# Moving a fifth of the dense experts' first products from the key loop to the end of the trunk

## The chip, the core and the metric

The kernel runs on one NeuronCore of a Trainium2 chip. TensorE (PE) multiplies matrices, VectorE (DVE) and ScalarE (ACT) do the element-wise work, GpSimd (POOL) issues the gathers, and the queue of SyncE (SP) issues most other transfers; 16 DMA engines carry them between the device memory (HBM) and on-chip memory. The metric is the device time of one execution in microseconds.

## The reference

One step of a hybrid layer over 9 tiles of 128 tokens (8 tiles of a prompt, one of decode samples), model width 1024. Cut to the part that matters here:

```python
x = x + mixer(rmsnorm(x, g_mix), ...)          # gating unit + retention: "the trunk"
t = rmsnorm(x, g_ffn)
q = (t @ w_query).reshape(T, 8, 256)           # 8 heads
s1, s2 = q[..., :128] @ k1.T, q[..., 128:] @ k2.T     # scores over 128 first and 128 second keys
v1, i1 = top_k(s1, 16); v2, i2 = top_k(s2, 16)
cand = (v1[..., :, None] + v2[..., None, :])          # 16 x 16 sums, of these the best 16
vals, flat = top_k(cand, 16)
experts = e1 * 128 + e2                        # one of 16384 single-neuron experts
w = softmax(vals)
a = gelu(einsum('td,thkd->thk', t, eu[experts]))      # first product, with u
out = einsum('thk,thkd->td', w * a, ev[experts])      # second product, with v
x = x + out;  y = rmsnorm(x, g_final)
```

## The kernel before

A tile framework takes the program as written, with priorities, and lays each engine's instructions out in one fixed order; every engine then runs its own list in order and waits on semaphores. [...]

**Trunk.** The tiles run in three groups (`GROUPS`, L48). `order` (L92 to L106) lists the 128 weight units of 512 x 256 for each group. `take` (L127 to L142) hands the next unit to the products: it keeps three raw loads ahead (`load`, L115 to L124, queued on SP) and splits each unit into a high and a low part, a cast on ACT and a subtraction on DVE (`split`, L197 to L206), since every product is the sum of three products of parts. The last step of a group is `query` (L597 to L630), 8 heads of scores; between the heads it runs `ahead`, the preparation of the next group's input, of which there is none for the last group.

**Experts, in two ways.** Tiles 0, 1, 2, 6 and 7 are *gathered*: for each of a token's 128 chosen experts an indirect DMA (L791) fetches the rows of u and v, DVE forms the dot product (L752), ACT the GELU and weight (L757, L758), DVE accumulates (L762). That is 640 gathers of 1 MB, through five buffers `gat`. Tiles 3, 4, 5 and 8 are *dense*: for each of the 128 second keys e all 128 experts of that key are computed for all 512 tokens. For this `expand` (L797 to L848) turns a tile's 128 choices per token into a full 128 x 128 table of weights: per four tokens one comparison on DVE (L828), four steps split between DVE (L838) and ACT (L842, L843) by `AA` (tokens 1 and 3 of four on DVE), four matmuls (L818), a copy to the buffer `st` (L819), and after four such chunks a 1 MB store of `st` to the spill `pdr` (L821). `st` is one buffer.

**The order around the change.** `advance(c)` moves a side clock by the matmul time just issued and lets two side lanes run up to it: the lane of gathers, one gather per `PACE` us, and the lane of top-16 and expansion (`topk_units`, L665 to L746), which after the trunk has priority. When the trunk is through, the four dense tiles are transposed to `tT` (L931 to L941), then the side lanes run until tile 8 is expanded (L942 to L944). Only then do the trunk's buffers close and the key loop begins (L1005 to L1047). For each key e it multiplies u of that key with `tT` into `S` (24 matmuls of 512 columns, L1014), takes GELU (L1019), multiplies by the weights `pt` (L1021, loaded from `pdr` for eight keys at a time, L1009), splits the result into `g`, splits u of key e + 2 and v of key e, and runs 24 matmuls of 512 columns with v (`res` and `blk`, L985) for the key before. Raw u and v pass through one ring of four slots `wraw` (L962 to L965). The block sums are added in L994.

Of the kernel before, what the change touches and what calls it, by code (L numbers as in the profile page):

```python
# [44 lines left out]

EARLY = [0, 1, 2, 8]
TD = len(DENSE) * P
EC = 4  # L48
LT = 16
BE = 8  # L50
# [4 lines left out]
def step_kernel(ctx: ExitStack, tc: tile.TileContext, x, state, wall, wst, bs, rows, vec, cst, smp, cosd, sind, euv,  # L55
# [37 lines left out]
    for g in range(len(GROUPS)):  # L93
# [10 lines left out]
            order += [U_IN + 2 * (32 + cb), U_IN + 2 * (32 + cb) + 1, U_PA + 2 * cb, U_PA + 2 * cb + 1]  # L104
        order += [U_OUT + i for i in range(8)] + [U_Q + i for i in range(16)]
    per = len(order) // len(GROUPS)  # L106
    NRAW, NPART, NBK = 3, 3, 2
    GB = 5
    MIX = 3
# [5 lines left out]
    def load(n):  # L115
        nonlocal pair
        if n < per - 2 and n % 3 < 2:

            if n % 3 == 0:
                pair = peer.tile([P, 2, 4, 256], F32, name="gat", bufs=GB)  # L120
            t = pair[:, n % 3]
        else:
            t = wp.tile([P, 4, 256], F32, name="wraw", bufs=NRAW)
        nc.sync.dma_start(t, wall[order[n]])  # L124
        return t

    def take():  # L127
# [94 lines left out]
    def front(gi, pl):  # L222

        tl = GROUPS[gi]
        nt = len(tl)
        xt = pl.tile([P, nt, D], F32, name="xt")
        ss = pl.tile([P, 4], F32, name="fss")
        junk = pl.tile([P, D], BF16, name="fjunk")
        for i, t in enumerate(tl):
            nc.sync.dma_start(xt[:, i], x[t])  # L230
        yield
        for i in range(nt):
            nc.scalar.activation(junk, xt[:, i], AF.Square, accum_out=ss[:, i:i + 1])
            rstd_of(ss[:, i:i + 1], ss[:, i:i + 1], D, epst)
            nc.scalar.activation(xt[:, i], xt[:, i], AF.Copy, scale=ss[:, i:i + 1])
            if i % 2:
                yield
        hT = hTs[gi] = pair_tiles(act, nt * P, "h")
        for k in range(KD):
            ps = sp.tile([P, 512], F32, name="sps")  # L240
            for i in range(nt):
                tr(ps[:, i * P:(i + 1) * P], xt[:, i, k * P:(k + 1) * P], ident)
            split([t[:, k] for t in hT], ps[:, :nt * P], vc[:, C_GMIX + k:C_GMIX + k + 1])
            if k % 2:
                yield

    def trunk(gi):
        tl = GROUPS[gi]
# [348 lines left out]
    def query(gi, pl, tl, nt, T, tT, rs, unit):  # L597
        def scores(h, qh):
            for i, t in enumerate(tl):
                ps = sp.tile([P, 2, P], F32, name="sps")  # L600
                for c in range(2):
                    mm(ps[:, c], qh[:, c, i * P:(i + 1) * P], sk[c], start=True, stop=True)
                st = pl.tile([P, 2, P], F32, name="st", bufs=2 * nt)
                nc.scalar.activation(st, ps, AF.Copy, scale=rs[:, i:i + 1])
                st = st.rearrange("p a b -> p (a b)")
                if t in EARLY:
                    top_keys(t, h, st)
                else:
                    store(ssp[t][:, h], st, 1)

        prev = None
        ahead = front(gi + 1, pl) if gi + 1 < len(GROUPS) else iter(())
        next(ahead, None)
        for h in range(PH):
            qh = pl.tile([P, 2, T], F32, name="qh", bufs=2)
            unit = unit or gemm_f(tT, T, U_Q + 2 * h)
            nc.scalar.copy(qh, (yield from unit))
            unit = None
            if prev:
                scores(*prev)  # L620
# [12 lines left out]
    BOOST = [100]  # L633
    AB = 2
    EUB, RWB = 2, 4
    AA = (1, 3)
    BB = (1, 0)
    EXC = 4
    DP = 200
# [157 lines left out]
    def expand(t):  # L797
# [27 lines left out]
        for c in range(P // EC):  # L825
            ab = ex.tile([P, 2, EC, P], F32, name="ab", bufs=AB)
            if c % BB[0] >= BB[1]:
                nc.vector.tensor_tensor(ab[:, 1], eT[:, 1, EC * c:EC * c + EC, None].to_broadcast([P, EC, P]),  # L828
                                        io[:, None, :].to_broadcast([P, EC, P]), op=OP.is_equal)
            else:  # L830
                for j in range(EC):
                    k = EC * c + j
                    nc.scalar.activation(ab[:, 1, j], io, AF.Square, scale=-1.0, bias=eT[:, 1, k:k + 1])
                nc.scalar.activation(ab[:, 1], ab[:, 1], AF.Relu, scale=-1.0, bias=1.0)
            for j in range(EC):
                k = EC * c + j
                if j % 4 in AA:
                    nc.vector.tensor_scalar(ab[:, 0, j], io, eT[:, 0, k:k + 1], eT[:, 2, k:k + 1],  # L838
                                            op0=OP.is_equal, op1=OP.mult)
                else:  # L840

                    nc.scalar.activation(ab[:, 0, j], io, AF.Square, scale=-1.0, bias=eT[:, 0, k:k + 1])  # L842
                    nc.scalar.activation(ab[:, 0, j], ab[:, 0, j], AF.Relu, scale=eT[:, 3, k:k + 1],  # L843
                                         bias=eT[:, 2, k:k + 1])
            if last:
                products(*last)
            last = c, ab
            yield EXC  # L848
# [67 lines left out]
    def advance(c):  # L916
        nonlocal tm
        tm += c
        flush()
        run_side(tm)  # L920
# [7 lines left out]
        ready.update(GROUPS[gi])  # L928


    prep = ExitStack()  # L931
    dx = prep.enter_context(tc.tile_pool(name="dx", bufs=2))
    tT = pair_tiles(act, TD, "h")
    for n, t in enumerate(DENSE):
        xt = dx.tile([P, D], F32, name="dx")
        nc.sync.dma_start(xt, tsp[t])
        for j in range(2):
            ps = sp.tile([P, 4, P], F32, name="sps")
            for k in range(4):
                tr(ps[:, k], xt[:, (4 * j + k) * P:(4 * j + k + 1) * P], ident)  # L940
            split([w[:, 4 * j:4 * j + 4, n * P:(n + 1) * P] for w in tT], ps)  # L941
    while len(expanded) < len(DENSE):  # L942
        tm += 1.0
        run_side(tm)  # L944
    prep.close()
    ex_sb.close()
    trunk_sb.close()
    trunk_ps.close()
# [12 lines left out]

    def fetch(name, e):  # L962
        if e < NKEYS:
            raw[name, e] = wp.tile([P, D], F32, name="wraw", bufs=RWB)
            nc.sync.dma_start(raw[name, e], eud[e].rearrange("p k e -> p (k e)") if name == "eu" else evd[e])  # L965

    def split_u(e):
        if e < NKEYS:
            eu[e] = [wp.tile([P, D], F32R, name=n, bufs=EUB) for n in ("whi", "wlo")]
            split(eu[e], raw.pop(("eu", e)))  # L970

# [22 lines left out]
            nc.vector.tensor_tensor(oacc[o], oacc[o], ps, op=OP.add)  # L994

    us = 24 * mm_us(TD)
    PACE[0] = 4.6
    todo = []
    hp = ExitStack()
    hp.enter_context(tc.high_priority(DP))  # L1000
# [4 lines left out]
    for e in range(NKEYS + 1):  # L1005
        if e < NKEYS:
            if e % BE == 0:
                pt = dp.tile([P, TD // LT, BE, LT], F32, name="pt", bufs=2)
                nc.sync.dma_start(pt.rearrange("p c e t -> p c (e t)"), pdr[e // BE])  # L1009
            ps = dps.tile([P, TD], F32, name="S")  # L1010
            for k in range(KD):
                w, a = [p[:, k * P:(k + 1) * P] for p in eu[e]], [p[:, k] for p in tT]
                for i, (x, y) in enumerate(((w[0], a[0]), (w[1], a[0]), (w[0], a[1]))):
                    mm(ps, x, y, start=k == 0 and i == 0, stop=k == KD - 1 and i == 2)  # L1014
            del eu[e]
            fetch("ev", e + 1)
            fetch("eu", e + 2)
            a = dp.tile([P, TD], F32, name="a", bufs=2)
            nc.scalar.activation(a, ps, AF.Gelu_apprx_tanh)  # L1019
            r16 = lambda z: z.rearrange("p (c t) -> p c t", t=LT)  # L1020
            nc.vector.tensor_tensor(r16(a), r16(a), pt[:, :, e % BE], op=OP.mult)  # L1021
            G[e] = [dp.tile([P, TD], F32R, name=f"g{m}", bufs=NBK + 1) for m in range(2)]
            split(G[e], a)
            split_v(e)
            split_u(e + 2)
            hp.close()
            advance(us)
            hp.enter_context(tc.high_priority(DP))
        if todo:
            block(*todo.pop())  # L1030
        if e:
            for o in held:
                value(res[o], o, e - 1, e == 1, e == NKEYS)
            if e % NBK == 0 or e == NKEYS:
                es = list(range((e - 1) // NBK * NBK, e))
                if len(blocked) > 0:
                    block(blocked[0], es)
                if len(blocked) > 1:
                    todo.append((blocked[1], es))
            hp.close()  # L1040
            advance(us)
            hp.enter_context(tc.high_priority(DP))
# [98 lines left out]
```

## Time and profile before

| | |
|---|---|
| median of 3 runs | 3904.63 us (3904.46 to 3918.01) |
| the profiled execution | 3911.42 us, span of its instructions 3909.7 us |
| busy in the span | PE 3583.4, DVE 3433.9, ACT 1838.5, POOL 986.5 us |
| DMA | 1176 MB, mean 301 GB/s |
| mean granted clock of PE | 0.962 of 2.4 GHz |

Times in the profile are microseconds from the span's start. An engine's busy time is the union of its instructions; a mean duration overlaps a little with the next instruction, so what one costs in a full stretch is read from start to start. "to landing" is the time from a DMA's issue to its last byte. Line numbers in the profile are those of the kernel before; the change shifts them by 4 in the weight stream, by 17 in the top-16 and the expansion, and by 30 in the key loop.

### The profile page before, as it was taken

How to read it: one execution, taken by the hardware profiler on the slowest of the kernel's cores; microseconds unless marked ns; L12 is line 12 of the kernel's file. 1: busy time of each engine (PE TensorE's matmuls, PEld its weight loads, DVE VectorE, ACT ScalarE, POOL GpSimd, SP SyncE). 2: the span in 40 equal slices, each digit the busy share in tenths (PEclk: the TensorE clock that was granted, in tenths of full speed). 3: DMA queues.
4: the chain of work that ended last, by engine and by line, in shares of the span. 5: the costliest groups of instructions: out<-in, count | busy, mean ns of one | idle time of the engine just before them, and what ended most of it. 6: DMA issues, size and time to landing. Idle time of an engine off the chain costs nothing.

```text
span 3909.7 us, 54608 instructions
## 1 busy us (share of the span) xinstructions
PE 3583.4 (92%) x19724; PEld 3060.1 (78%) x19724; DVE 3433.9 (88%) x6391; ACT 1838.5 (47%) x3839; POOL 986.5 (25%) x692
## 2 busy tenths in 40 slices
PE   8999999999999888889989836999999999999998
PEld 6789977887877787878989835777787777777776
DVE  5666799999988899899888897999999999899996
ACT  4445634444443545656666637343344343343443
POOL 0000002333433220221212221233223333333331
PEclk9999999999999999999999967999999999999999
DMA  8766547999989874685868965899789999999995
GB/s 313 248 238 200 179 161 297 377 343 349 364 315 361 343 273 145 238 288 182 296 213 310 315 240 199 326 381 370 274 317 367 391 376 386 346 388 373 380 383 187
DMA packets 243759, 1176.00 MB, mean 301 GB/s; under 512 B 26656, under 2 KB 43808, under 8 KB 159520
## 3 DMA queue, kind: packets, MB, share of 16 engines
q0 software_dynamic: 105216, 721.46, 49.5%
q1 hardware_dynamic: 138272, 451.04, 31.5%
q8 instruction: 155, 2.54, 0.3%
q14 instruction: 116, 0.95, 0.1%
HBM read 1095.86 MB, written 76.55 MB: 300 GB/s over the span
## 4 chain that ended last, share of the span: by engine, by line
issue 33%; PE 19%; DVE 17%; POOL 15%; DMA 12%; ACT 4%; POOLq 0%; SPq 0%; DVEq 0%; ACTq 0%
POOL gat L791 15%; PE gps L176 6%; DMA pdr<-st 4%; PE S L1014 4%; PE gps L192 3%; DMA gat<-in_euv_dram,idx 3%; DVE wlo L204 3%; DVE acc L762 2%; PE res L985 2%; DVE gat L752 2%; PE blk L985 1%; DMA s<-ssp 1%; DVE ktmp L646 1%; ACT whi L200 1%; ACT st L819 1%
## 5 line engine op out<-in xcount | busy, mean ns | idle before, releaser
L791 POOL DMA_INDIRECT gat<-in_euv_dram,idx x640 | 935.4, 1462 | 2395.9 <-DVE acc L762 1651.9
L752 DVE CUSTOM_DVE_ANT_0 gat<-gat,tx 128x1024 f32<-128x1024 f32 x640 | 777.8, 1216 | 69.5 <-DMA gat<-in_euv_dram,idx 51.9
L762 DVE SCALAR_TENSOR_TENSOR acc<-gat,sdot,acc 128x1024 f32<-128x1024 f32 x640 | 816.9, 1276 | 0.8 <-ACT sdot L758 0.6
L985 PE MATMUL res<-ev,g 128*128 128x512 f32 x2304 | 802.0, 392 | 11.1 <-ACT g L200 10.9
L1014 PE MATMUL S<-h,whi 128*128 128x512 f32 x2048 | 758.6, 398 | 9.6 <-ACT st L819 5.3
L192 PE MATMUL gps<-whi,h 128*128 128x256 f32 x3456 | 660.4, 290 | 5.2 <-ACT whi L200 1.9
L204 DVE TENSOR_TENSOR wlo<-wraw,whi 128x1024 fp32r<-128x1024 f32 x428 | 520.7, 1217 | 91.8 <-ACT whi L200 90.5
L200 ACT CAST whi<-wraw 128x1024 fp32r<-128x1024 f32 x428 | 447.3, 1045 | 263.0 <-PE gps L176 140.3
L192 PEld LDWEIGHTS gps<-whi,h 128*128 128x128 f32 x3456 | 556.2, 196 | 18.4 <-issue 11.8
L985 PEld LDWEIGHTS res<-ev,g 128*128 128x128 f32 x2304 | 432.6, 189 | 114.3 <-ACT g L200 21.0
L757 ACT ACTIVATE sdot<-sdot 128x1 f32<-128x1 f32 x640 | 128.1, 202 | 837.3 <-DVE sdot L752 835.7
L192 PE MATMUL gps<-wlo,h 128*128 128x256 f32 x1728 | 500.9, 290 | 20.7 <-DVE wlo L204 20.7
L176 PE MATMUL gps<-h,whi 128*128 128x256 f32 (+2 forms) x1920 | 498.7, 342 | 10.4 <-ACT pb L330 5.8
L1014 PEld LDWEIGHTS S<-h,whi 128*128 128x128 f32 x2048 | 387.6, 189 | 118.7 <-ACT a L1019 34.3
L176 PE MATMUL gps<-y,whi 128*128 128x256 f32 (+2 forms) x1536 | 399.0, 342 | 21.4 <-ACT y L202 9.9
L1014 PE MATMUL S<-h,wlo 128*128 128x512 f32 x1024 | 402.1, 393 | 0.0
L176 PEld LDWEIGHTS gps<-h,whi 128*128 128x128 f32 x1920 | 343.9, 193 | 37.2 <-ACT pb L330 6.0
L192 PEld LDWEIGHTS gps<-wlo,h 128*128 128x128 f32 x1728 | 338.4, 196 | 30.1 <-DVE wlo L204 22.4
L176 PE MATMUL gps<-h,wlo 128*128 128x256 f32 (+2 forms) x960 | 328.1, 342 | 8.1 <-DVE wlo L204 8.1
L176 PEld LDWEIGHTS gps<-y,whi 128*128 128x128 f32 x1536 | 272.6, 191 | 47.5 <-ACT y L202 10.8
L200 ACT CAST ev<-wraw 128x512 fp32r<-128x512 f32 x256 | 158.0, 622 | 258.0 <-PE res L985 128.4
L176 PE MATMUL gps<-y,wlo 128*128 128x256 f32 (+2 forms) x768 | 261.3, 341 | 2.2 <-DVE wlo L204 2.1
(216 smaller groups left out, 5132.5 us busy)
## 6 DMA issues: line engine op xcount, KB each, us to landing
wraw<-in_wall_dram SPq DMA_DIRECT2D x300, 512.0 KB, 5.6
wraw<-in_eud_dram SPq DMA_DIRECT2D x128, 512.0 KB, 7.7
wraw<-in_evd_dram SPq DMA_DIRECT2D x128, 512.0 KB, 7.6
gat<-in_wall_dram SPq DMA_DIRECT2D x84, 512.0 KB, 4.7
pdr<-st POOLq DMA_DIRECT2D x32, 1024.0 KB, 7.8
pt<-pdr SPq DMA_DIRECT2D x16, 2048.0 KB, 11.9
Sb<-in_state_dram SPq DMA_DIRECT2D x16, 1024.0 KB, 6.9
out_dram<-Sb POOLq DMA_DIRECT2D x16, 1024.0 KB, 7.8
```

The lines of the kernel that those rows point to most:

```text
L176: mm(ps[:, c, :T], x, y, start=kh == 0 and k == 0 and j == 0, stop=kh == nk - 1 and k == 3 and j == len(pr) - 1)
L192: mm(ps[:, i], y, x, start=kh == 0 and k == 0 and j == 0 and i % 2 == 0, stop=kh == 1 and k == 3 and j == len(pr) - 1 and last)
L200: nc.scalar.copy(parts[0], src)
L204: nc.vector.tensor_tensor(parts[1], src, parts[0].bitcast(F32), op=OP.subtract)
L646: nc.vector.match_replace(tmp, v[:, :8], src, -3.0e38)
L752: nc.vector.tensor_tensor_reduce(out=b[:, :D], in0=b[:, :D], in1=d["x"], op0=OP.mult, op1=OP.add, scale=1.0, scalar=0.0, accum_out=d["s"][ ...
L757: nc.scalar.activation(d["s"][:, j:j + 1], d["s"][:, j:j + 1], AF.Gelu_apprx_tanh)
L762: nc.vector.scalar_tensor_tensor(d["acc"], b[:, D:], d["s"][:, j:j + 1], d["acc"], op0=OP.mult, op1=OP.add)
L791: nc.gpsimd.indirect_dma_start(out=b, out_offset=None, in_=euv, in_offset=bass.IndirectOffsetOnAxis(ap=d["idx"][:, j:j + 1], axis=0))
L819: nc.scalar.copy(st[:, :, EC * r:EC * (r + 1)].rearrange("p e t -> p t e"), ps)
L985: mm(ps, x, y, start=start and i == 0, stop=stop and i == 2)
L1014: mm(ps, x, y, start=k == 0 and i == 0, stop=k == KD - 1 and i == 2)
```

## The change

The first `NU` = 26 keys' u are appended to the weight stream, so that `take` loads and splits them like trunk units. The dense tiles are transposed by `turn_dense`, which takes the empty place of `ahead` in the last group's query heads. A new loop behind the trunk multiplies the 26 keys with `tT`, in the trunk's PSUM tiles, takes GELU and spills 256 KB per key to `gdr`. In the key loop the first 26 keys load that spill through the `wraw` ring in place of u and have no product, no GELU and no split of u, and advance the side clock once instead of twice. The pace of gathers there is 6.5, from key 26 on 4.4, in place of 4.6. For tile 8 three of four tokens' expansion steps go to DVE (`AL`) in place of two.

```diff
+NU = 26
+    order += [("eu", e) for e in range(NU)]
-        nc.sync.dma_start(t, wall[order[n]])
+        u = order[n]
+        nc.sync.dma_start(t, wall[u] if isinstance(u, int) else eud[u[1]].rearrange("p (a k) e -> p a (k e)", a=4))
+    def turn_dense(pl):
+        tT = hTs["dense"] = pair_tiles(act, TD, "h")
+        for n, t in enumerate(DENSE):
+            xt = pl.tile([P, D], F32, name="dx", bufs=2)
+            nc.sync.dma_start(xt, tsp[t])
+            yield
+            for j in range(2):
+                ps = sp.tile([P, 4, P], F32, name="sps")
+                for k in range(4):
+                    tr(ps[:, k], xt[:, (4 * j + k) * P:(4 * j + k + 1) * P], ident)
+                split([w[:, 4 * j:4 * j + 4, n * P:(n + 1) * P] for w in tT], ps)
-        ahead = front(gi + 1, pl) if gi + 1 < len(GROUPS) else iter(())
+        ahead = front(gi + 1, pl) if gi + 1 < len(GROUPS) else turn_dense(pl)
-    AA = (1, 3)
+    AA, AL = (1, 3), (1, 2, 3)
-                if j % 4 in AA:
+                if j % 4 in (AA if t not in GROUPS[-1] else AL):
...
+    def first(ps, w):
+        for k in range(KD):
+            pr = products([z[:, k * P:(k + 1) * P] for z in w], [z[:, k] for z in tT])
+            for i, (x, y) in enumerate(pr):
+                mm(ps, x, y, start=k == 0 and i == 0, stop=k == KD - 1 and i == len(pr) - 1)
+    gdr = dr.tile([NU, P, TD], F32, name="gdr")
+    with tc.tile_pool(name="pu", bufs=3) as pl:
+        for e in range(NU):
+            _, w = take()
+            ps = sp.tile([P, TD], F32, name="sps")
+            first(ps, [z.rearrange("p a b -> p (a b)") for z in w])
+            a = pl.tile([P, TD], F32, name="gu")
+            nc.scalar.activation(a, ps, AF.Gelu_apprx_tanh)
+            store(gdr[e], a, 1)
+            advance(24 * mm_us(TD))
+        flush(True)
     while len(expanded) < len(DENSE):
...
+            elif e < NU:
+                nc.sync.dma_start(r[:, :TD], gdr[e])
...
-        if e < NKEYS:
+        if NU <= e < NKEYS:                      # in split_u
...
-    PACE[0] = 4.6
+    PACE[0] = 6.5
...
+            if e < NU:
+                ga = raw.pop(("eu", e))[:, :TD]
+            else:
+                ps = dps.tile([P, TD], F32, name="S")
+                first(ps, eu.pop(e))
...
-            nc.vector.tensor_tensor(r16(a), r16(a), pt[:, :, e % BE], op=OP.mult)
+            nc.vector.tensor_tensor(r16(a), r16(ga), pt[:, :, e % BE], op=OP.mult)
...
+            if e == NU:
+                PACE[0] = 4.4
+            if e >= NU:
+                hp.close()
+                advance(us)
+                hp.enter_context(tc.high_priority(DP))
```

The order that results is shown at three places. On PE, after the last query head (L602), the kernel before has the dense tiles' transposes (L940), the three transposes of tile 8's choices and weights (L801 to L803), all its expansion matmuls and then the first product of the key loop (L1014):

```order
L602 MATMUL sps<-vc,qh 128x128 x12
L940 MATMUL sps<-cs,dx 128x128 x32
L801 MATMUL sps<-cs,e_21794 128x128
L802 MATMUL sps<-cs,e_21794 128x128
L803 MATMUL sps<-cs,wp 128x128
L818 MATMUL sps<-ab 128x128 x128
L1014 MATMUL S<-h_21653,whi 128x512
```

In the change 72 of the new products (L954) stand between the last query head and the second of these transposes (L819, the weights' is L820); this is the piece that follows, with the expansion's matmuls (L835):

```order
L954 MATMUL sps<-h_20754,wlo 128x512
L954 MATMUL sps<-h_20755,whi 128x512
L819 MATMUL sps<-cs,e_21845 128x128
L820 MATMUL sps<-cs,wp 128x128
L835 MATMUL sps<-ab 128x128 x5
L954 MATMUL sps<-h_20754,whi 128x512
L954 MATMUL sps<-h_20754,wlo 128x512
L954 MATMUL sps<-h_20755,whi 128x512
L835 MATMUL sps<-ab 128x128
L954 MATMUL sps<-h_20754,whi 128x512
L835 MATMUL sps<-ab 128x128 x6
```

Of the 624 products 265 stand among the 128 expansion matmuls and 287 behind the last of them.

On DVE, in the key loop of the kernel before, from the multiplication of key 12 by its weights (L1021), there are a split of u (`wlo`), a split of g, dots (L752) and accumulations (L762) of gathers, and block sums (L994):

```order
L1021 TENSOR_TENSOR a<-a,pt 128x512
L204 TENSOR_TENSOR wlo<-wraw,whi 128x1024
L204 TENSOR_TENSOR g_23683<-a,g_23682 128x512
L752 ISA gat,sdot<-gat,tx 128x1024
L752 ISA sdot 128x1
L762 SCALAR_TENSOR_TENSOR acc<-gat,sdot,acc 128x1024
L752 ISA gat,sdot<-gat,tx 128x1024
L752 ISA sdot 128x1
L994 TENSOR_TENSOR oacc_22420<-oacc_22420,blk 128x512
L762 SCALAR_TENSOR_TENSOR acc<-gat,sdot,acc 128x1024
L752 ISA gat,sdot<-gat,tx 128x1024
L752 ISA sdot 128x1
```

In the change, at a multiplication in about the same place (L1052, which reads the loaded spill `wraw`), two keys follow each other closely; L208 is the split, L779 the accumulation, L1024 the block sum, L769 the dot:

```order
L208 TENSOR_TENSOR g_24162<-a,g_24161 128x512
L208 TENSOR_TENSOR ev_24170<-wraw,ev_24169 128x512
L1052 TENSOR_TENSOR a<-wraw,pt 128x512
L208 TENSOR_TENSOR g_24212<-a,g_24211 128x512
L208 TENSOR_TENSOR ev_24220<-wraw,ev_24219 128x512
L1024 TENSOR_TENSOR oacc_23546<-oacc_23546,blk 128x512
L779 SCALAR_TENSOR_TENSOR acc<-gat,sdot,acc 128x1024
L208 TENSOR_TENSOR ev_24260<-wraw,ev_24259 128x512
L1052 TENSOR_TENSOR a<-wraw,pt 128x512
L769 ISA gat,sdot<-gat,tx 128x1024
```

Counted over the whole order: from the multiplication of key 1 to that of key 25 the kernel before has 63 dots and the change 30; ahead of that stretch 312 and 337; behind it 265 and 273.

On SP, at the join of trunk and key loop, the kernel before loads the scores of a gathered tile, the weights pt, and u and v of the first keys:

```order
L677 DMA s_22643<-ssp_103 128x256
L1009 DMA pt<-pdr 128x4096
L965 DMA wraw<-in_eud_dram 128x1024
L965 DMA wraw<-in_evd_dram 128x1024
L965 DMA wraw<-in_eud_dram 128x1024
L1009 DMA pt<-pdr 128x4096
```

In the change the spills (L161) are stored in turn with the last loads of u (L128), and the first pt stands behind the last spill:

```order
L161 DMA gdr<-gu 128x512
L128 DMA wraw<-in_eud_dram 128x1024 x2
L161 DMA gdr<-gu 128x512 x4
L993 DMA wraw<-gdr 128x512 x2
L991 DMA wraw<-in_evd_dram 128x1024 x2
L161 DMA gdr<-gu 128x512
L1039 DMA pt<-pdr 128x4096
```

The load of pt has moved behind a store that waits for the 26th GELU.

## Rows read from the trace of the kernel before

**Rows 1.** The page: busy times of the span, and its slices.

```profile
PE 3583.4 (92%) x19724; PEld 3060.1 (78%) x19724; DVE 3433.9 (88%) x6391; ACT 1838.5 (47%) x3839; POOL 986.5 (25%) x692
...
DVE  5666799999988899899888897999999999899996
...
PEclk9999999999999999999999967999999999999999
```

**Rows 2.** Busy time by stage; the columns are in the first line.

```profile
core 0: us, PE busy (x) PEld busy (x) DVE busy (x) ACT busy (x) POOL busy (x), PEclk, DMA share, GB/s
2215.00:2273.80 58.80, 53.40 (x327) 53.02 (x327) 56.56 (x152) 28.81 (x69) 22.99 (x15) 0.97 0.95 341
2273.80:2332.00 58.20, 8.43 (x35) 7.02 (x35) 50.91 (x165) 13.46 (x33) 10.36 (x7) 0.50 0.65 251
2332.00:2416.00 84.00, 48.75 (x256) 44.44 (x256) 68.29 (x278) 73.00 (x168) 10.21 (x9) 0.74 0.41 121
...
2900.00:3830.00 930.00, 907.24 (x3901) 727.19 (x3900) 888.38 (x1186) 371.38 (x874) 342.42 (x233) 0.99 0.97 377
3830.00:3893.00 63.00, 62.97 (x273) 50.21 (x273) 35.57 (x49) 18.31 (x35) 1.81 (x2) 1.00 0.36 126
...
2273.80:2716.20 442.40, 344.87 (x1509) 280.31 (x1510) 397.81 (x841) 202.46 (x462) 118.57 (x84) 0.87 0.79 300
```

**Rows 3.** DVE in order of time: start, duration, instruction, idle time before it.

```profile
2273.78 0.34 DVE L693 TENSOR_TENSOR cand<-v 128x192 f32<-128x192 f32 x1
...
2435.81 1.29 DVE L1021 TENSOR_TENSOR a<-a,pt 128x512 f32<-128x512 f32 x2 [1.20 <-DMA pt<-pdr]
```

**Rows 4.** DVE in order of time, around the multiplication of key 25.

```profile
2716.16 0.68 DVE L1021 TENSOR_TENSOR a<-a,pt 128x512 f32<-128x512 f32 x1
2716.98 1.23 DVE L204 TENSOR_TENSOR wlo<-wraw,whi 128x1024 fp32r<-128x1024 f32 x1
2718.12 0.68 DVE L204 TENSOR_TENSOR g<-a,g 128x512 fp32r<-128x512 f32 x1
2718.72 1.28 DVE L762 SCALAR_TENSOR_TENSOR acc<-gat,sdot,acc 128x1024 f32<-128x1024 f32 x1
2719.92 1.22 DVE L752 CUSTOM_DVE_ANT_0 gat<-gat,tx 128x1024 f32<-128x1024 f32 x1
...
2721.06 1.28 DVE L762 SCALAR_TENSOR_TENSOR acc<-gat,sdot,acc 128x1024 f32<-128x1024 f32 x1
```

**Rows 5.** DVE in order of time, a chunk of the expansion.

```profile
2341.28 0.67 DVE L828 TENSOR_TENSOR ab<-eT,cs 128x512 f32<-128x512 f32 x1
2341.87 0.60 DVE L838 TENSOR_SCALAR ab<-cs,eT 128x128 f32<-128x128 f32 x2
2342.38 0.08 DVE L646 MATCH_VALUE_LOAD ktmp<-v,s 128x8 f32 x1
```

**Rows 6.** POOL in order of time: first and last of seven stores of tile 8.

```profile
2343.04 1.22 POOL L821 DMA_DIRECT2D pdr<-st  x1 [27.04 <-ACT ab L842]
...
2405.23 1.15 POOL L821 DMA_DIRECT2D pdr<-st  x1 [8.85 <-ACT ab L842]
```

**Rows 7.** DMA issues, us to landing last: 2330-2415, 1800-2300, 2900-3800 (two), 2416-2448.

```profile
pdr<-st POOLq DMA_DIRECT2D x7, 1024.0 KB, 6.1
...
pdr<-st POOLq DMA_DIRECT2D x15, 1024.0 KB, 11.9
...
wraw<-in_evd_dram SPq DMA_DIRECT2D x78, 512.0 KB, 7.8
...
pt<-pdr SPq DMA_DIRECT2D x9, 2048.0 KB, 12.0
...
wraw<-in_evd_dram SPq DMA_DIRECT2D x2, 512.0 KB, 14.5
```

**Rows 8.** ACT in order of time: four copies to st in a row.

```profile
2349.17 3.66 ACT L819 COPY st<-sps 128x512 f32<-128x512 f32 x4 [1.10 <-DMA pdr<-st]
```

More of the change, by code (lines that the diff above doesn't have):

```diff
@@ L928, in step_kernel @@
         ready.update(GROUPS[gi])
[L931 to L941, printed above, removed]
+    tT = hTs.pop("dense")
+    def first(ps, w):
[14 more added lines that the diff above has]
+        flush(True)
     while len(expanded) < len(DENSE):
@@ L944, in step_kernel @@
         run_side(tm)
-    prep.close()
     ex_sb.close()
@@ L963, in fetch @@
         if e < NKEYS:
-            raw[name, e] = wp.tile([P, D], F32, name="wraw", bufs=RWB)
-            nc.sync.dma_start(raw[name, e], eud[e].rearrange("p k e -> p (k e)") if name == "eu" else evd[e])
+            r = raw[name, e] = wp.tile([P, D], F32, name="wraw", bufs=RWB)
+            if name == "ev":
+                nc.sync.dma_start(r, evd[e])
+            elif e < NU:
+                nc.sync.dma_start(r[:, :TD], gdr[e])
+            else:
+                nc.sync.dma_start(r, eud[e].rearrange("p k e -> p (k e)"))
     def split_u(e):
-        if e < NKEYS:
+        if NU <= e < NKEYS:
             eu[e] = [wp.tile([P, D], F32R, name=n, bufs=EUB) for n in ("whi", "wlo")]
@@ L1009, in step_kernel @@
                 nc.sync.dma_start(pt.rearrange("p c e t -> p c (e t)"), pdr[e // BE])
[L1010 to L1015, printed above, removed]
+            a = dp.tile([P, TD], F32, name="a", bufs=2)
+            if e < NU:
+                ga = raw.pop(("eu", e))[:, :TD]
+            else:
+                ps = dps.tile([P, TD], F32, name="S")
+                first(ps, eu.pop(e))
             fetch("ev", e + 1)
             fetch("eu", e + 2)
-            a = dp.tile([P, TD], F32, name="a", bufs=2)
-            nc.scalar.activation(a, ps, AF.Gelu_apprx_tanh)
+            if e >= NU:
+                ga = a
+                nc.scalar.activation(a, ps, AF.Gelu_apprx_tanh)
             r16 = lambda z: z.rearrange("p (c t) -> p c t", t=LT)
-            nc.vector.tensor_tensor(r16(a), r16(a), pt[:, :, e % BE], op=OP.mult)
+            nc.vector.tensor_tensor(r16(a), r16(ga), pt[:, :, e % BE], op=OP.mult)
             G[e] = [dp.tile([P, TD], F32R, name=f"g{m}", bufs=NBK + 1) for m in range(2)]
@@ L1025, in step_kernel @@
             split_u(e + 2)
-            hp.close()
-            advance(us)
-            hp.enter_context(tc.high_priority(DP))
+            if e == NU:
+                PACE[0] = 4.4
+            if e >= NU:
+                hp.close()
+                advance(us)
+                hp.enter_context(tc.high_priority(DP))
         if todo:
```

## The prediction

> **What bounds the kernel now.** I read the busy table and the slices first [rows 1]: PE is busy 92% of the span and DVE 88%, and in one place, at about six tenths of the span, PEclk falls to 6 and 7. The stage table [rows 2] takes that place apart. Until 2273.8 the trunk's last projection fills PE. Then PE works 8.43 of 58.2 us while DVE does tile 8's top-16, its clock granted at 0.50 (1.2 of 2.4 GHz), and 48.75 of 84 us while tile 8 is expanded (0.74). After that the 128 keys run: from 2900 to 3830 PE, DVE and DMA are all near full (907, 888 of 930 us, DMA share 0.97). In the 63 us without gathers PE executes 273 matmuls, 0.231 us each; with gathers 3901 in 930 us, 0.238 each. So PE binds a key there, with DVE and the DMA engines 2 to 5% behind it.
>
> The stretch that the change rewrites runs from the first candidate sum of tile 8 (2273.78) to the multiplication of key 25, the last of the 26 (2716.16) [rows 3, 4]. I call it J: 442.4 us, of which PE 344.9, DVE 397.8, DMA share 0.79 [rows 2]. Outside J the instruction order is nearly the old one, so the sum is made for J, with small terms at both ends.
>
> **The parts.** *What is moved on PE.* 26 keys times 24 products of 512 columns, 624 matmuls, 624 x 0.238 = 149 us, leave the key loop for J's idle PE (442.4 - 344.9 = 97.5 us). They fit only partly: of the 624, 72 stand ahead of the transpose of tile 8's weights, 265 among the expansion's matmuls and 287 behind its last one. PE runs in order, so it still stands idle through most of the top-16.
>
> *What DVE has to do in J.* The spacing of instructions back to back gives the price of one [rows 4, 5]: gather dot 1.14, accumulation 1.20, split of 1024 columns 1.14, any 512-column step 0.60, the expansion's 128-column step 0.51 / 2 = 0.255. Between the same two marks the new order has 8 of the dense transposes' steps less (-4.8), 4 splits of u less (-4.6), 6 splits of v less (-3.6), 6 dots and 5 accumulations less (-6.8, -6.0), 3 block sums less (-1.8), 32 expansion steps more (+8.2, the new AL) and some nine small top-16 steps more (about +1.8): -17.6. DVE's work in J falls from 397.8 to 380.2 us. It is only 17.6 us less, since the splits of u are moved inside J, not removed. This is the floor that PE's 149 us can't get under.
>
> *J stage by stage.* (a) Top-16: the order has 12 gathers where 7 stood, and the 8 transposes' steps are gone: 50.9 + 5 x 2.34 - 4.8 = 57.8 us of DVE, at full occupation about 60 (58.2 before). The stops for the dense tiles' loads go, so this is all work. (b) Expansion: DVE 68.3 + 32 x 0.255 + 10 x 1.14 + 4 x 1.14 + 7 x 1.20 - about 1.8 = 99 us, at the 95.5% that DVE reaches between 2900 and 3830 about 104. The other limit is the one buffer st: seven stores leave at 10.4 us apart [rows 6] with 6.1 us to landing [rows 7], so a block costs landing + 4.3, most of it the four copies (3.66 us) that wait for the store [rows 8]. Such a store took 11.9 us in the busier trunk [rows 7]; now gathers, u and spills run beside it, at a load between the two. I take 9.0, halfway: 8 x 13.3 = 106 us. (84 before.) ACT, 73.0 of 84 us busy, gives a quarter of its square-and-relu pairs to DVE and takes casts and GELUs of about ten keys for it; I count it at nothing. PE needs 265 x 0.238 = 63 and the expansion's own 48.75 x 0.74 = 36 us there, 99 at the full clock; 134 at the 0.74 that it had while 58% busy, 28 more than I count. It was 0.99 where PE was as busy as it would now be [rows 2], so I take the full clock. (c) The 287 matmuls behind it: 68.5 us, in which DVE has the top-16 of a gathered tile and about 20 gathers. (d) The join: pt is queued on SP behind the last spill, which waits for the last GELU; 12.0 us to landing [rows 7], with GELU, trigger and stop about 17 (19.8 before, from 2416 to 2435.81). What stands behind that wait on SP are the next loads of the key loop; PE waits for it with DVE working gathers off. (e) From key 0 to key 25: PE 25 x 24 x 0.238 = 143 us; DVE 30 gathers x 2.34 + 114 steps x 0.60 = 139, at 95.5% 145; DMA 25 x (0.52 MB of v + 0.26 spilled + 0.26 of pt) + 30 gathers x 1.05 MB = 57.7 MB, at 377 GB/s [rows 2] 153 us. DMA ends last: 153, or 6.1 a key (280.4 before, from 2435.81 to 2716.16).
>
> Sum of the stages: 60 + 106 + 68.5 + 17 + 153 = 404.5. The DVE floor at the best occupation seen, 380.2 / 0.955 = 398, is close to it, and both would have to be met at once. At the 89.9% of J before, DVE needs 423. Between 404.5 and 423 I take 408 (DVE at 93%), nearer to the first, because the stage that pulled the 89.9% down, the expansion with DVE at 81%, now has DVE as a limit. J saves 442.4 - 408 = 34.4.
>
> *The ends.* Ahead of J the dense tiles' transposes now run inside the query heads, where DVE works 56.6 of 58.8 us [rows 2]: 8 x 0.60 + 3 x 1.14 - 2 x 2.34 = +4. Behind J 273 gathers are left for the same 102 keys instead of 265; six of the eight fall into the last keys, where DVE works 35.6 of 63 us and DMA is at 0.36 [rows 2], two into full stretches: +4. The spill itself, 13.6 MB written and read, is 36 us of all DMA engines at 377 GB/s; the write lies under the DMA share of 0.41 of the expansion, the read stands in (e). The two other paces (6.5, then 4.4) only set where gathers stand, which the counts hold already.
>
> Net: 34.4 - 8 = 26.4 us. The profiled execution took 3911.4 us, 1.7 more than its span; it would take 3885. It lies 6.8 above the median of the runs shown, so the median goes from 3904.6 to **3878**, 0.7% faster.
>
> *Two rules against it.* In the key loop PE is busy 97.6% but its weight loads only 78% (727 of 930) [rows 2]. Perfetto Trace Analysis (§ Identifying the Most-Contended Engine) of the Trainium skill holds matmul busy time for a bad measure and wants the share of the weight loads; by it TensorE has room in the loop, the moved matmuls are worth nothing there, and only DVE's 17.6 us count: 17.6 - 8 = 9.6 us, 3895. The gather-free row speaks for PE: with DVE half idle a matmul still took 0.231.
> The 930 us carried 377 GB/s. DMA: Bandwidth & Descriptors (§ Where 436 GB/s comes from) of the Trainium skill lets HBM bind a core at about 358 GB/s; by it (e) would take 161 us instead of 153, and the sum would be 3886. The trace goes above that figure for a quarter of the span, so I keep 377.
>
> **The rivals.** *The store cycle holds the expansion.* With 11.9 us to landing, as among the trunk's loads [rows 7], a block costs 16.2 us and the expansion 130, 24 more than counted; ACT stands in order before the copies, so splits and GELUs wait as well, and DVE stays as idle in J as it was. 26.4 - 24 = 2.4: 3902. For it: before, the landing nearly doubled under load. Against: the load here is lower than there. A clock that stays at 0.74 in the expansion would cost about the same (28) and is counted with it.
>
> *Slower: the four-slot ring of raw tiles in keys 0 to 25.* One 512 KB tile of v and one spilled tile pass through four slots at half the old period, so a slot is refilled only after the key two before it was split: two periods = landing + about 2.4 us (four half-tile steps at 0.6). At the 7.8 us to landing of the full loop this gives 5.1 us a key and binds nothing; at the 14.5 of the old join, where a 2 MB pt was loaded beside it [rows 7], 8.45 us a key, 211 us for (e), 58 more: 3936. It makes the change slower by more than 0.5% from 13.5 us to landing on (8.0 us a key). The new stretch asks for 2.31 MB per 6.1 us, which is the rate of the full loop, where landings stayed at 7.8; that is against it.
>
> *PE was the only limit.* Then J shrinks to PE's 344.9: 97.5 - 8 = 89.5 us, 3815. DVE's 380.2 us of work forbids most of it; half of it, 3860, is already inside the forecast's range.
>
> **How the numbers follow.** Forecast 0.56, with its own range 3850 (DVE at 100%: 442.4 - 380.2 - 8 = 54 saved) to 3890; store cycle 0.28 (3890 to 3920); ring 0.10; PE alone 0.06. One can tell 0.5%, 19.5 us, from no change: under 3885 is faster, over 3924 slower. Faster: nearly all of the forecast's 0.56, the 0.06, together 0.60. Same: the store cycle and the forecast's upper edge, 0.30. Slower: 0.10. The range 3848 to 3915 leaves out the ring, PE alone and a little of the store cycle.
>
> **What would show it.** In the profile after: PE idle until about 2335 as before, with three keys' products at the start; stores of tile 8 at 13 us apart, not 10.4 (16 for the first rival); the last product of the 26 keys at about 2510; key 0 multiplied at about 2530; 6.1 us from key to key up to key 25 (8 and more for the ring), 11.4 after it (48 x 0.238). DVE at about 93% from the top-16 to key 25. If DVE idles over 10% there, I am wrong in the occupation; if PE waits for v or the spilled tiles, in the ring; if the keys from 26 on take longer than 11.6 us, in the ends.

## The result and the profile after

The changed kernel takes 3930.47 us (median of 10 runs, 3925.09 to 3944.05), the kernel before beside it 3905.78: a ratio of 1.0065, 95% interval 1.0048 to 1.0082. It is 0.65% slower, where 0.7% faster was forecast, and the time lies outside the range. The profiled execution has a span of 3928.3 us, 18.6 more than before.

The page, engines and slices (answers to [rows 1]):

```profile
PE 3576.2 (91%) x19724; PEld 3057.5 (78%) x19724; DVE 3442.5 (88%) x6423; ACT 1818.4 (46%) x3775; POOL 978.8 (25%) x692
...
DVE  5666799999898799898898898877999999999998
...
PEclk9999999999999999999999879899999999999999
```

PE's clock has two shallow dips (8 and 7 in slices 23 and 24, 8 in slice 26) for one deep one (6 and 7 in slices 24 and 25), and DVE has fallen from 9 to 7 in slices 27 and 28, counted from 1. By stage (answers to [rows 2]; same columns):

```profile
core 0: us, PE busy (x) PEld busy (x) DVE busy (x) ACT busy (x) POOL busy (x), PEclk, DMA share, GB/s
2278.00:2338.00 60.00, 17.53 (x70) 13.87 (x69) 59.20 (x171) 16.88 (x43) 20.14 (x12) 0.64 0.70 261
2338.00:2450.00 112.00, 97.44 (x514) 82.21 (x514) 94.02 (x286) 68.31 (x127) 22.46 (x17) 0.94 0.73 235
2450.00:2517.00 67.00, 63.61 (x275) 52.24 (x274) 63.27 (x143) 23.72 (x49) 22.61 (x14) 0.97 0.79 283
2517.00:2548.50 31.50, 0.95 (x5) 0.45 (x3) 19.12 (x33) 6.26 (x19) 7.33 (x6) 0.60 0.99 401
2548.50:2725.30 176.80, 143.21 (x554) 111.95 (x555) 141.25 (x206) 54.11 (x131) 42.59 (x31) 0.91 0.86 327
2725.30:2750.00 24.70, 20.95 (x85) 16.53 (x84) 19.37 (x42) 8.18 (x16) 2.16 (x3) 0.93 0.80 311
2750.00:2900.00 150.00, 140.84 (x596) 112.33 (x595) 140.40 (x350) 56.30 (x114) 29.95 (x22) 0.98 0.76 275
```

Top-16, expansion (second row) and the remaining products (third) go about as planned. Then come three rows that are longer than planned: 31.5 us (the join) in which PE does nothing and the DMA engines are full, 26 keys at 7.07 us with PE and DVE both busy for four fifths, and 24.7 us from key 25 to key 26. The mark of a key is the start of its multiplication by the weights on DVE. The marks of J and of what follows (answers to [rows 3] and [rows 4]), DVE in order of time:

```profile
2275.79 0.55 DVE L710 TENSOR_TENSOR cand<-v 128x192 f32<-128x192 f32 x2
...
2548.48 1.29 DVE L1052 TENSOR_TENSOR a<-wraw,pt 128x512 f32<-128x512 f32 x2
...
2716.41 0.69 DVE L1052 TENSOR_TENSOR a<-wraw,pt 128x512 f32<-128x512 f32 x1 [1.58 <-DMA wraw<-gdr]
2725.31 0.68 DVE L1052 TENSOR_TENSOR a<-wraw,pt 128x512 f32<-128x512 f32 x1
...
2749.87 0.68 DVE L1052 TENSOR_TENSOR a<-a,pt 128x512 f32<-128x512 f32 x1
```

J is 2725.31 - 2275.79 = 449.5 us for 442.4 before, with key 26 behind it by 24.56 for 11.45. The 18.6 us are 2.0 ahead of J, 7.1 in J, 13.1 from key 25 to key 26, and -3.6 from there to the end. In J, DVE is busy for 379.1 us, which is the work that was counted (380.2), but at 84% and not at 93%.

The chain of waits in the join (start, us, what; SPq is the queue of SP):

```profile
2509.79 8.17 PE sps L954 x36
...
2519.36 0.48 SPq L991
2519.93 19.59 DMA gdr<-gu
2539.58 0.63 ACT ev L204
```

The last spill, 256 KB, takes 19.59 us to land among the loads of the first keys and the gathers, at 401 GB/s. ACT's first copy of v waits for it, and so does the load of pt, which SP issues at 2539.78. The chain in the keys:

```profile
2695.20 0.69 DVE ev L208
2695.91 6.05 DMA wraw<-gdr
2702.05 0.69 DVE a L1052
...
2710.38 0.62 DVE ev L208
2711.01 5.31 DMA wraw<-gdr
2716.41 0.69 DVE a L1052
```

A spilled tile is loaded only when DVE's difference of an earlier v has freed a slot. It lands 5 to 6 us later, its key is multiplied, and 8 us of DVE's work later the next difference frees a slot. That is 15.1 us for two keys. The queue of SP in 2548 to 2750 says the same (waited for: us in total, times, longest):

```profile
SPq L993 <- DVE ev L208: 70.7, 16, 9.0
SPq L991 <- DMA wraw<-gdr: 45.1, 11, 6.3
```

L993 loads the spilled tiles, L991 v. Each stands in turn behind the other's slot.

### The profile page after: what moved, and what is told of

Its sections match the earlier page's. It is cut to its first block, busy times and chain, and to the rows that moved or that the text cites. A ratio compares the mean times of both kernels' runs of the same rounds, so it can differ in the third digit from the quotient of the medians.

```text
span 3928.3 us, 54767 instructions
## 1 busy us (share of the span) xinstructions
PE 3576.2 (91%) x19724; PEld 3057.5 (78%) x19724; DVE 3442.5 (88%) x6423; ACT 1818.4 (46%) x3775; POOL 978.8 (25%) x692
## 4 chain that ended last, share of the span: by engine, by line
issue 30%; PE 22%; DVE 18%; DMA 13%; POOL 13%; ACT 4%; POOLq 0%; SPq 0%; DVEq 0%; ACTq 0%
POOL gat L808 13%; PE gps L180 6%; DMA pdr<-st 4%; PE S L954 4%; PE gps L196 3%; PE res L1015 3%; DVE acc L779 3%; DVE wlo L208 3%; DMA gat<-in_euv_dram,idx 3%; DVE gat L769 2%; DMA wraw<-gdr 1%; PE blk L1015 1%; PE sps L954 1%; ACT whi L204 1%; ACT st L836 1%
## 5 line engine op out<-in xcount | busy, mean ns | idle before, releaser
L769 DVE CUSTOM_DVE_ANT_0 gat<-gat,tx 128x1024 f32<-128x1024 f32 x640 | 779.1, 1218 | 55.7 <-DMA gat<-in_euv_dram,idx 44.9
L779 DVE SCALAR_TENSOR_TENSOR acc<-gat,sdot,acc 128x1024 f32<-128x1024 f32 x640 | 817.9, 1278 | 1.7 <-ACT sdot L775 1.3
L1015 PE MATMUL res<-ev,g 128*128 128x512 f32 x2304 | 772.8, 396 | 41.9 <-ACT g L204 40.0
L954 PE MATMUL S<-h,whi 128*128 128x512 f32 x1632 | 605.5, 398 | 12.0 <-ACT a L1050 8.2
L208 DVE TENSOR_TENSOR wlo<-wraw,whi 128x1024 fp32r<-128x1024 f32 x428 | 521.4, 1218 | 94.7 <-ACT whi L204 93.6
L954 PEld LDWEIGHTS S<-h,whi 128*128 128x128 f32 x1632 | 308.5, 189 | 99.8 <-ACT a L1050 32.1
L954 PE MATMUL S<-h,wlo 128*128 128x512 f32 x816 | 320.0, 392 | 0.0
L1015 PE MATMUL blk<-ev,g 128*128 128x512 f32 x768 | 243.3, 405 | 42.9 <-DVE oacc L1024 39.0
```

Source lines behind the costliest of these rows:

```text
L208: nc.vector.tensor_tensor(parts[1], src, parts[0].bitcast(F32), op=OP.subtract)
L769: nc.vector.tensor_tensor_reduce(out=b[:, :D], in0=b[:, :D], in1=d["x"], op0=OP.mult, op1=OP.add, scale=1.0, scalar=0.0, accum_out=d["s"][ ...
L779: nc.vector.scalar_tensor_tensor(d["acc"], b[:, D:], d["s"][:, j:j + 1], d["acc"], op0=OP.mult, op1=OP.add)
L1015: mm(ps, x, y, start=start and i == 0, stop=stop and i == 2)
```

## The experiments

"Ratio" is that to the kernel before on the same chip, with its 95% interval. Two questions were put: is it the ring, or the bytes as such (E1 to E5); and what are the keys beyond the expansion worth (E6, E7, E11, E12).

**E1, slots of their own for the spilled tiles.**

```diff
+            if name == "eu" and e < NU:
+                r = raw[name, e] = wp.tile([P, D], F32, name=("whi", "wlo")[e % 2], bufs=EUB)
+                nc.sync.dma_start(r[:, :TD], gdr[e])
+                return
...
-            elif e < NU:
-                nc.sync.dma_start(r[:, :TD], gdr[e])
```

> The u results of keys 0 to 25 are loaded into the four slots of the split parts of u (two of whi, two of wlo, idle until key 26); the four raw slots hold loads of v alone. Nothing else is edited. Theory 1, the ring: a load of the changed kernel waits until one of four raw slots is free, mostly by the difference of v (wraw<-gdr is the largest piece of the chain in keys 0 to 25), so with twice the slots the 176.8 us from key 0's multiplication to key 25's fall to 150 to 160, key 26's multiplication follows key 25's by 11 to 14 instead of 24.6, since its raw u no longer queues for a slot, and the join stays at 31; the time is about 3930 - 20 - 12 = 3898. Theory 2, the load itself: 57.8 MB pass in those 176.8 us with the DMA engines busy for 0.86; landings stay long whatever the slots, the 26 keys take 170 or more, only key 26 gains, and the time is 3915 to 3930.

Measured: 3907.76 us, ratio 1.0002 (0.999 to 1.0014). Stage of the 26 keys, then key 25 to key 26:

```profile
2549.40:2692.90 143.50, 134.09 (x554) 104.49 (x555) 139.22 (x207) 53.33 (x129) 42.61 (x30) 0.97 1.00 394
2692.90:2708.40 15.50, 12.67 (x56) 10.05 (x55) 12.50 (x28) 4.51 (x9) 3.89 (x2) 1.00 0.84 319
```

With about the same matmuls and DVE steps, 176.8 us become 143.5: DVE is busy for 97%, the DMA engines for 1.00 at 394 GB/s. Key 26 follows after 15.5 us instead of 24.7. The ring is shown as the cause for both, and the bytes as such are not: they pass faster once there is room for them. The slowdown is gone; the join is no shorter (38 us: the last GELU starts at 2511.37 for 2517.98, and key 0 stands where it was). The whole gain is 22 us, not 33 + 9, because the mark on DVE runs ahead of PE: from 2278 to 2900 PE works 20.1 us more than in the changed kernel (504.60 for 484.52).

**E2, the wait for the last spill taken away; E3, both edits; E4, pt early as well.** E2's edit, and E4's beside it:

```diff
-    dp = dense_sb.enter_context(tc.tile_pool(name="dp", bufs=1))
+    dp = dense_sb.enter_context(tc.tile_pool(name="dp", bufs=1, reuse_waits="tile"))
```

```diff
+    pp = ctx.enter_context(tc.tile_pool(name="pp", bufs=1, side="right"))
...
-                pt = dp.tile([P, TD // LT, BE, LT], F32, name="pt", bufs=2)
+                pt = pp.tile([P, TD // LT, BE, LT], F32, name="pt", bufs=2)
```

> The pool with pt and the split parts of v lands on the bytes of the spill's tiles; in the changed kernel all its tiles wait for every user of those bytes, here each tile waits only for the users of its own bytes. The order of every engine is that of the changed kernel. Theory 1, the wait for the last spill: pt's load is issued at 2520 to 2522 instead of 2539.8, ACT copies v from about 2522 instead of 2539.6, and key 0's multiplication comes 12 to 17 us earlier; the keys behind keep their 7 us each, so the time is about 3916. Theory 2, the DMA load in the join (engines busy for 0.99 at 401 GB/s): pt's 2 MB land no earlier than they do now, the wait moves from the spill to pt, and the time stays within 3 us of 3930.

> Both edits before: the u results in the slots of whi and wlo, and tiles that wait only for the users of their own bytes. Theory 1, ring and spill are two causes that add: join 31 to 17, keys 176.8 to 150-160, key 26 11 to 14 behind: about 3930 - 14 - 20 - 12 = 3884, 22 below the kernel before. Theory 2, one load that every wait shares: what one edit gives the other takes, 3905 to 3925.

> Both edits, and pt in a pool of its own at the other end of the memory, so that the loads of its first two groups (2 MB each) are issued while the last products are still running, as soon as the last dense tile's stores have landed, instead of in the join. Theory 1, pt's landing is what the join keeps once the spill is out of it: the join falls to 8-10 us, and the time is 8 below that of both edits alone, about 3876. Theory 2, the load of the DMA engines: the 4 MB only move from the join into the products' stage, where the weight stream then waits; the time is within 3 us of both edits alone.

Measured: E2 3924.28 us, ratio 1.0039 (1.0026 to 1.0053); E3 3904.51, 0.9989 (0.9976 to 1.0001); E4 3901.77, 0.9982 (0.9969 to 0.9995). E2's SP, and then its DVE at key 0:

```profile
2522.63 0.38 SPq L161 DMA_DIRECT2D gdr<-gu  x1
2523.31 0.33 SPq L1039 DMA_DIRECT2D pt<-pdr  x1
```

```profile
2549.80 1.29 DVE L1052 TENSOR_TENSOR a<-wraw,pt 128x512 f32<-128x512 f32 x2 [2.49 <-DMA pt<-pdr]
```

The load of pt is issued 16 us earlier and lands no earlier: key 0 comes 29.1 us after the last GELU, 30.5 before. The wait named in the chain was not what the join costs, since another load at the same full DMA engines took its place. Theory 1 falls for the join. The time lies between the two theories, 6 us below the changed kernel's median (10 by the ratios). The two intervals just meet, and E2's profiled execution (3931.94 us) is the longest of its runs, so how much of it is real, and where, stays open. E3 is far from the 3884 of its theory 1: on top of the slots, the waits bring nothing that can be measured. E4 lies within the 3 us of its theory 2. In E4 pt is there early and key 0 follows the last GELU by 15 us, but the loads of v and the last spill (22.12 us to landing) still share the join, and key 1 comes only at 2554.39.

**E5, the raw tiles early too.** Their pool moves to the other end of the memory as well, and eight loads are issued from the products' loop:

```diff
...
+    dw = dense_sb.enter_context(tc.tile_pool(name="dw", bufs=1, side="right"))
...
+    first8 = [(n, e) for e in range(4) for n in ("eu", "ev")]
...
+            if 0 <= e - NU + 9 < 8:
+                fetch(*first8[e - NU + 9])
```

> E4 and, beside it, the raw tiles at the other end of the memory too: the loads of u results and of v for keys 0 to 3 (3 MB) and of the first group of pt (2 MB) are issued while products and expansions run; the spill has two tiles instead of three. Theory 1, the join is the time that its bytes take (12.6 MB in 31.5 us at 401 GB/s in the changed kernel): with 5 MB gone from it, key 0's multiplication follows the last product by 8 us or less, TensorE sits idle for 5 to 12 us there instead of 30, and the time is 15 to 25 below that of E3 (both edits, 3904.5), about 3885. Theory 2, the DMA engines are short of time in the whole stage, not in the join alone: the products are delayed by what is moved among them, and the time is within 5 us of E4 (3901.8).

Measured: 3890.77 us, ratio 0.9963 (0.9951 to 0.9975). Its stages from the products behind the expansion to key 25:

```profile
2450.00:2517.00 67.00, 63.52 (x267) 51.50 (x266) 61.98 (x122) 24.25 (x51) 20.44 (x13) 0.95 0.84 315
2517.00:2523.00 6.00, 0.17 (x1) 0.00 (x0) 5.00 (x8) 2.15 (x7) 1.86 (x2) 0.76 1.02 426
2523.00:2667.80 144.80, 134.74 (x555) 105.05 (x556) 140.23 (x208) 54.42 (x131) 41.64 (x30) 0.96 0.98 394
```

Key 0 comes 5.8 us after the last GELU. What is loaded early costs the products little: from tile 8's first candidate sum to the last GELU it is 244.4 us in E5, 247.3 in E8 (alike up to there) and 248.7 in E4, for 236.9 to 242.2 in the changed kernel and E1 to E3, which load nothing early. So the join was the time of its bytes, in a place where nothing else could run; the stage before had room for most of them. From 2278 to 2900 the changed kernel and then E5:

```profile
2278.00:2900.00 622.00, 484.52 (x2091) 389.57 (x2090) 536.63 (x1223) 233.76 (x498) 147.24 (x103) 0.90 0.79 290
```

```profile
2278.00:2900.00 622.00, 532.94 (x2332) 423.85 (x2331) 577.94 (x1272) 251.83 (x536) 157.78 (x110) 0.93 0.83 313
```

PE works 48.4 us more, and the span is 43.3 shorter. By the medians E5 is 14 us below E3, a little under the 15 to 25 of theory 1.

**E8, E9: is it VectorE that hands the gain back?** The mark of key 26 moves by 67 us in E5 and the end by 43.

```diff
         for j in range(HK):
+            if t == GATHER[-1] and HK - 14 <= j < HK - 1:
+                continue
```

> E5 without 13 of the 64 gathers of the last gather tile (the positions 50 to 62 are left out of its sum), which is what VectorE has left over at key 26 against the kernel before (73 gathers done by then, 85 before). Of the 67 us by which E5 brings key 26 forward against the changed kernel (2682.7 for 2749.9) only 43 reach the end. Theory 1, the rest is given back to VectorE, which now ends last (last gather 3850.7, last key 3853.9; in the kernel before 3846.6 and 3887.5): without 13 x 2.5 = 32 us of its work the time falls by 15 to 25, to about 3870. Theory 2, TensorE bounds what follows key 26 and the rest is its backlog: the time falls by 5 or less.

> The kernel before without the same 13 gathers: the price of 32 us of VectorE's work where TensorE ends last. Theory 1, VectorE ends last only where stages ahead have been shortened: the kernel before falls by 5 or less, clearly less than E5 does. Theory 2, both engines share the tail in every kernel: it falls by as much as E5, 10 or more.

The edit leaves out positions 114 to 126 of that tile's 128, not 50 to 62 of 64. Measured: E8 3890.79 us, ratio 0.9958 (0.9942 to 0.9974), E5 without the edit 0.9963; E9 3908.55, 1.0003 (0.9992 to 1.0014). Some 30 us of DVE's work less (13 x 2.34) change nothing that can be measured in either. Theory 1 falls: VectorE does not end last in either kernel. TensorE does, busy for 940.3 of the 955 us from 2900 to 3855 in E5.

What seemed handed back has two parts. By the mark of the last key E5 is 52.4 us ahead (3853.91 for 3906.35), so 15 of the 67 were DVE's mark running ahead of PE. The other 9 are lost behind the last matmul, which ends at 3915.63 in the changed kernel and at 3862.86 in E5. The queue of SP there, its first load of x and the last wait ahead of it, for the changed kernel and then E5:

```profile
3905.71 0.33 SPq L1085 DMA_DIRECT2D dx<-xsp  x1
...
SPq L1085 <- PE S L954: 0.9, 1, 0.9
```

```profile
3862.90 0.33 SPq L1095 DMA_DIRECT2D dx<-xsp  x1
...
SPq L1095 <- PE blk L1025: 5.8, 1, 5.8
```

The last load of x (`dx`) waits for the last product with u in the changed kernel, 10 us before the last matmul ends, and for the last matmul itself in E5. From the last matmul to the end it is 21.8 to 22.2 us in all five kernels with E5's edits and 12.7 to 13.0 in all others. Which of the edits moves this wait was not tested. The moved pool of the raw tiles is a candidate, since `dx` takes memory that the key loop's pools give up (argued, not shown).

**E10, the change's other edit undone in E5.**

```diff
-    AA, AL = (1, 3), (1, 2, 3)
+    AA, AL = (1, 3), (1, 3)
```

> E5 with two of four columns of the last dense tile's expansion on VectorE, as in the kernel before, instead of three (AL = AA): 32 x 0.367 = 11.7 us off VectorE, 32 x (0.396 + 0.490) = 28 us more on ScalarE, in the stage 2338 to 2450 where VectorE is busy for 96 and ScalarE for 68 of 112 us. If VectorE is what ends last (theory 1), the time falls by up to 10, to about 3882; if the expansion's chain through ScalarE and the weights' copies decides (theory 2), the expansion takes 5 to 15 longer and the time rises to 3895 to 3905.

Measured: 3903.05 us, ratio 0.9984 (0.9971 to 0.9997) for E5's 0.9963. Theory 2 is what the median says: VectorE's third column is worth about 0.2%, 8 us. The two intervals overlap a little, so the size is open.

**E7, E12, E6, E11: fewer keys ahead.** NU = 16 and 20 in the changed kernel (E7, E12) and in E5 (E6, E11).

> The changed kernel with 16 keys ahead instead of 26, nothing else edited. Theory 1, the ring costs each key ahead a time (7.07 us a key where PE and DVE have 5.6 of work) and the join and the late u of the first key behind once: 10 keys fewer give back about 10 x 1 to 1.5 us, join (31) and the late u (24.6) stay, and the time is 3915 to 3922. Theory 2, the products that follow the expansion are worth their time: the time rises above 3930.

> The changed kernel with 20 keys ahead instead of 26, nothing else edited; E7 had 16 (3895.7), the changed kernel 26 (3930). Theory 1, each key ahead behind the expansion costs its own share, a product of 6.2 us and a key of 7 to 7.5 against one of 11.4, so the time is linear in their number, 3.5 us a key: 3910, and the edits of E11 (3885.0 with 20 keys) are worth 25. Theory 2, the loss sits in one place (join, late u of the first key behind) and not in the keys: 3925 or more. If slots and early loads don't matter with fewer keys: 3885 to 3890, as E11.

> E5 with 16 keys ahead instead of 26. If products beyond the last dense tile's expansion (2450 us) gain nothing, since the expansion no longer hides them, and only cost a store and a load of 256 KB each, the time is that of E5 or up to 6 us below. If every product ahead gains, because the later keys without one run faster, it is 5 to 15 us above E5.

> E5 with 20 keys ahead instead of 26. The ends are E5 (26: 3890.8) and E6 (16: 3895.3). If what follows the expansion is neutral, the time lies between them, 3889 to 3896; if there is an optimum between, because products beyond the expansion cost a spill and a reload while fewer than about 18 leave TensorE idle in it, 3883 to 3889.

| keys ahead | the change alone | with E5's edits |
|---|---|---|
| 16 | E7: 3895.66, 0.9974 (0.9962 to 0.9985) | E6: 3895.34, 0.9983 (0.9972 to 0.9994) |
| 20 | E12: 3903.29, 0.9994 (0.998 to 1.0008) | E11: 3884.99, 0.9943 (0.9927 to 0.9958) |
| 26 | 3930.47, 1.0065 (1.0048 to 1.0082) | E5: 3890.77, 0.9963 (0.9951 to 0.9975) |

E7 came out 20 us below what either theory expected. Each key fewer gave 3.5 us, not 1 to 1.5. By the marks: from 16 to 26 keys the last GELU moves from 2456.0 to 2517.98, 6.2 us a product. Keys 15 to 25 are multiplied in 75.5 us (2649.79 to 2725.31), 7.55 each. So a key ahead costs 13.7 us behind the expansion, where an ordinary one costs E7 11.4 (keys 16 to 26 in 113.5 us). I had left the product out of the price. The other 12 us of E7's 36 at key 26 are a shorter join (27) and shorter first keys (6.2 each). E12 lies between, 2 us a key (by the ratios) up to 20 and 4.6 beyond. So theory 2, one loss in one place, falls; theory 1 is nearer, but its 3.5 us for every key is an average of the two. In E7, join and late u of the first key behind (24.0 us) are still there.

With the ring and the join mended, 20 keys are best of the three: E11 beats the kernel before by 0.57% and E5 by about 0.2%, though these two intervals overlap a little. With 16 keys the edits bring nothing that can be measured, and E6 fits neither of its expectations (5 us above E5). Its trace shows the shorter join (last GELU 2455.66, key 0 at 2465.6) and PE working 23 us more than E7's by 2900. Its last matmul ends 16.2 us earlier than E7's (3870.60 for 3886.79), and 9 of these are lost behind it, as in E5. E7's profiled execution is also 6 us above its median, so little is left.

## Why the prediction was wrong

By its own steps, from the changed kernel's trace; the parts add up to 449.5 where 404.5 was summed and 408 taken.

- **(a) top-16**, 60: 62. **(c) the products behind**, 68.5: 68, with the last one at 2518 for 2510. Right.
- **(b) expansion**, 106: 112. The mechanism was right and the size a little off: tile 8's stores came at 2345.17 to 2449.96, 15.0 us apart for 13.3, although they landed in 8.3 us (9.0 taken). The landing was not what was undercounted. The four copies, 3.66 us in a row before [rows 8], are now spread, since they wait for their matmuls in PE's order among the products and stand in ACT's among casts and GELUs. ACT's first and fourth copy of the last block, with a GELU between them that waits for PE:

```profile
2437.74 1.01 ACT L836 COPY st<-sps 128x512 f32<-128x512 f32 x1 [5.21 <-DMA pdr<-st]
...
2446.78 0.60 ACT L964 ACTIVATE gu<-sps 128x512 f32<-128x512 f32 x1 [4.45 <-PE sps L954]
...
2448.22 1.09 ACT L836 COPY st<-sps 128x512 f32<-128x512 f32 x1
```

- **The first rival, the store cycle**, did not come: 112 and not 130. PE's clock was granted at 0.94 in that stage, near the full clock that was taken.
- **(d) join**, 17: 30.5. This step failed. It took pt's 12.0 us to landing from the full loop and put GELU and trigger ahead of it. Here the last spill and pt passed with the first loads of all slots and the gathers, 12.6 MB in 31.5 us at a DMA share of 0.99, and pt lands 26 us after its issue where nothing else holds it (E2). The join of the kernel before had shown longer landings too: of its two loads of pt the one issued at 2430.38 took 20.7 us. The wait for the spill, which the sum did not have, was real in the trace; without it the join took 29.1 us for 30.5 (E2).
- **(e) key 0 to key 25**, 153: 176.8. This is the step that failed most. Its bounds were near (with free slots E1 takes 143.5, with the DMA engines at 1.00 and 394 GB/s for the 377 taken), but it took the slowest engine where a loop of waits decided. The rival "four-slot ring" named the mechanism, and its equation mis-sized one term: two periods = landing + 2.4 us of half-tile steps. The landing was 5 to 6 us in the chain, no more than the 7.8 that I had taken; the other term was 8 to 9, since between a multiplication and the next difference that frees a slot DVE does, in order, dots, accumulations and a block sum. With 6 + 9 in place of 7.8 + 2.4 the rival gives 7.5 us a key (measured 7.07). I had weighed it by the landing alone and gave it 0.10.
- **Key 26**, taken as an ordinary 11.4: 24.6. It was not in the sum. The first key with its own u got its raw tile through the same four slots, issued at 2726.02, after key 25's multiplication. E1 brought this to 15.5.
- **The ends**: +2.0 ahead of J for +4, and -3.6 behind key 26 for +4. Neither is clear of what executions differ by. At the first mark, up to which E9 is the kernel before, the two differ by 6 us (2267.89 and 2273.78); from key 26 to the end the kernel before takes 1182.1 us and E9, with less work there, 1191.5. Beside the rest the ends are small.
- **DVE's floor** of 380.2 us was right as work and did not set J's time. DVE was at 91% from 2278 to 2517 and at 61% and 80% in the two stages behind it.
- **What is left**: with ring and join mended E5 still takes 3890.8 for the 3878 forecast; 9.5 of these 13 us stand behind its last matmul, an estimate from 22.2 us there in E5 and 12.7 in the changed kernel.
- **PE as the limit** of the loop is borne out: with some 30 us less of DVE's work neither E5 nor the kernel before gains (E8, E9), while 48.4 us more of PE's work by 2900 brought E5's last matmul forward by 52.8 and shortened its span by 43.3. Perfetto Trace Analysis (§ Identifying the Most-Contended Engine) of the Trainium skill goes by the share of the peak rate reached and by the share of the weight loads. The second is 78% here [rows 2] and would have given TensorE room; these runs don't agree with it.

What the sum never asked: what a product is worth where PE is not idle. By its own numbers a key whose product stands behind the expansion cost 5.7 for the product and 6.1 for the key against 11.2 before (280.4 us for 25), so those twelve were forecast to lose 0.6 us each; measured 2.4 (13.7 for 11.4, from the changed kernel and E7).

## What to carry to other kernels

When work is moved so that a loop's period is halved, go round each ring of buffers once: landing, plus everything that the engine does in order between the use and the release, over the periods that the slots allow. The slowest engine is only the lower bound. A join where loads of the next stage, a spill and a big table start together costs the time of their bytes, whichever wait the chain names; start them in the stage before, in memory that is already free, and take away the bytes, not the wait. And move only as much as the idle time holds: the rest pays for its spill. After moving a pool, look at the loads behind the loop too: what they wait for can change.

## What the hardware showed unexpectedly

A store of 256 KB took 19.59 us to land in the join of the changed kernel, and 22.12 in E4's; the DMA share was 1.02 and 0.96 while they were under way. 2 MB of pt took 26 us in E2's join, at 1.02, and 12.0 in the full loop of before, at 0.97. The engines carried 401 GB/s in the join of the changed kernel and 394 over the 26 keys of E1, with 377 in the full loop before [rows 2]. DMA: Bandwidth & Descriptors (§ Where 436 GB/s comes from) of the Trainium skill lets HBM bind a core at about 358 GB/s, half of a stack's figure for two cores; with one core at work the runs went above it.
